# Two more halves of the adaLN vectors summed on VectorE, in two other places of the stream, with six stream buffers in place of seven

## The chip, the cores and the metric

The kernel runs on one core of one Trainium2 chip. The metric is the device time of one execution in microseconds (us), as a median of several runs; lower is better.

## What is computed

One decoder block on 256 tokens of width 2048, in float32. What matters here is the conditioning ahead of it and the order of the large products:

```
cond = silu(c)
ada = cond @ w_ada + b_ada                    # 2048 -> 6 * 2048
sh1, sc1, gt1, sh2, sc2, gt2 = split(ada, 6)
u = rmsnorm(h) * (1 + sc1) + sh1
proj = u @ w_in                               # queries, keys/values, gates, S5 input, merge gates
y_a = sparse attention(...)
y_b = GLU(S5 scan(...))
h = h + gt1 * ((g_a * y_a + g_b * y_b) @ w_out)
u2 = rmsnorm(h) * (1 + sc2) + sh2
h = h + gt2 * (relu(u2 @ w_up)^2 @ w_down)
out = rmsnorm(h)
```

sc1 and sh1 are wanted first, since the whole projection waits for u. gt1, sh2 and sc2 (the "later vectors") are wanted only when w_out's product ends. gt2 has code of its own, which the change doesn't touch.

## The kernel before, in words

**The stream.** All weights pass through one list of *units*. A unit loads one tile `raw` of 128x1024 float32 (512 KB) on SyncE's DMA queue and then does something with it. There are RAW = 7 such buffers, and the load of a unit is issued RAW units ahead (two fewer while the S5 outputs run, which borrow two buffers). `run_units` (L244) walks the list; its order is the order of work on every engine's queue.

**Main units** (`gemm=True`) split the weights in two: ScalarE copies `raw` to `hi` (L117), VectorE writes `lo = raw - hi` (L120), and TensorE does three products per tile of weights (L316, L318, L319, or L923 to L925 for the values, where weights and activations change sides). TensorE's part of a unit is put in its queue SPLIT = 2 main units later. `hi` and `lo` have three buffers each.

**Units without a split** (`gemm=False`) are the adaLN vectors and the compression of keys and values. For the later vectors there are six halves of 1024 columns: half h is vector h // 2 (gt1, sh2, sc2), columns 1024 * (h % 2) on. A half takes 16 tiles in either of two ways:

- `ada2_pe_units` (L1046, TensorE): the tiles come in pairs. For each pair, 16 products of 128 columns (L1060) go into one PSUM bank, ScalarE copies the bank to a stage, and after every fourth pair four transposes (L1069) and a sum on VectorE finish 512 columns.
- `ada2_units` (L973, VectorE): each tile, 128 rows of w_ada, is multiplied by the 128 values of `cond` and added to a 128x1024 accumulator, one instruction of VectorE a tile (a `tensor_scalar` for the first, L124, then 15 `scalar_tensor_tensor`, L129). At the end TensorE sums over the partitions (L991), ScalarE copies, and TensorE transposes (L1000).

Which half goes which way stands in a tuple, and how many tiles go into which stage in a list:

```
RAW, HI, LO = 7, 3, 3
ADA2 = [0, 16, 16, 16, 32, 16]
ADA_PE = (0, 1, 3, 4, 5)
...
units += weave(proj_units(C_GA, d_g, 0, AF.Tanh, 0.5, True), some())
```

`some()` hands out the next ADA2 tiles, `weave` spreads them over the main units of a stage. The six stages before are: the end of the values with the S5 inputs (mark E), the merge gates of A (ga), the queries (q), the merge gates of B (gb), the GLU (glu), the output product (out). So half 0 lies in ga, half 1 in q, half 2 (on VectorE) in gb, halves 3 and 4 in glu, half 5 in out.

**What lies around the change.** The first pass goes over w_in in five chunks of rows, since u comes in pieces; each chunk has four passes (two of S5 input, one of compressed keys/values, one of keys), and each pass ends with four sums of a PSUM bank into SBUF on VectorE (`RX<-A`, for the keys `st<-A` with a store to DRAM on ScalarE's queue). The last chunk has 16 main units. Then come the values (mark vs; 16 main units, 8 units of compression woven in), and from mark E on, with the last six of them and the gate unit, the S5 inputs.

*Background generators* put other work between units. Those that matter: `p2` (S5 operands, copies at L741, up to 8 units ahead of vs, counted in units), `xw` (x^T stored to DRAM on GpSimd's queue, at vs - 20), `cmp` (sums for the compression, at vs - 2), `lam` (`s5_lambda`, twelve 128x1024 operations of VectorE, after vs), `keep` (stores of d_c on SyncE's queue, L786), `stk` and `in` (S5 inputs: SBUF to SBUF copies on GpSimd's queue, L809, products L835, and four ScalarE copies a step), and `attn` (attention, during glu).

Of the kernel before, what the change touches and what calls it, by code (L numbers as in the profile page):

```python
# [23 lines left out]
    0, 2048, 3072, 3584, 4096, 4608, 5120, 5168, 7216, 9264)  # L24
A_SH1, A_SC1, A_GT1, A_SH2, A_SC2, A_GT2 = (i * D for i in range(6))

RAW, HI, LO = 7, 3, 3
SPLIT = 2
ADA2 = [0, 16, 16, 16, 32, 16]
ADA_PE = (0, 1, 3, 4, 5)  # L30
SCAN_END = 0.4
ATTN_WAIT = 5
AS0, AS1 = 2, 13
# [48 lines left out]
def block_kernel(ctx, tc, cst_in, x, c, w_ada, b_ada, g_mix, w_in, w_ck2, pe_ck,  # L82
# [21 lines left out]
    def big4():  # L104
        return sp.tile([128, 1024], FT, tag="s4", name="s4", bufs=2)
# [79 lines left out]
    units = []  # L185
# [231 lines left out]
    def first_pass_units(ci):  # L417
        k0, k1 = chunks[ci]
        res = []
        for g in PASS:  # L420
            def finish(b, ps, g=g):
                acc = part[g][:, b * 512:(b + 1) * 512]
                if ci == 0:
                    copy(acc, ps)
                elif ci < len(chunks) - 1 or g < 3:
                    tt(acc, ps, acc, OP.add)
                else:
                    st = stage()
                    tt(st, ps, acc, OP.add)
                    A.dma_start(out=d_k[:, 2 * b:2 * b + 2, :], in_=st.rearrange("p (k t) -> p k t", k=2))  # L430
            kw = dict(halves=l_keys) if g == 3 else {}
            col0 = (C_SSM, C_SSM + 1024, C_KC, 0)[g]
            res += gemm_pass(w_in[0], col0, list(range(k0, k1)), 1024, True, True, (uh, ul), BA, finish, joint=J_P1 if ci >= J_P1C else 1, **kw)
        return res
# [476 lines left out]
    def vs_units():  # L911
        made = {}

        def run(u, kt):
            if kt == 0:
                made["b"] = [bank(t) for t in BA]
            lo = u.lo
            for t in range(2):
                xh, xl = uh[:, kt, t * 128:t * 128 + 128], ul[:, kt, t * 128:t * 128 + 128]
                for s in range(2):  # L920
                    o = made["b"][2 * t + s]
                    at = slice(512 * s, 512 * s + 512)
                    PE.matmul(out=o, lhsT=xh, rhs=u.hi[:, at], start=kt == 0, stop=False)  # L923
                    PE.matmul(out=o, lhsT=xl, rhs=u.hi[:, at], start=False, stop=False)
                    PE.matmul(out=o, lhsT=xh, rhs=lo[:, at], start=False, stop=kt == 15)  # L925
                    if kt == 15:
                        st = stage()
                        copy(st, o)
                        A.dma_start(out=d_v[:, t, s, :], in_=st)
        return [Unit([(lambda r: r, l_vals[kt])], lambda u, k=kt: run(u, k)) for kt in range(16)]  # L930

    def gate_unit():
        def run(u):
            ps = bank("T0")
            h3 = u.hi.rearrange("p (k n) -> p k n", n=48)
            l3 = u.lo.rearrange("p (k n) -> p k n", n=48)
            for kt in range(16):
                o = ps[0:48, 0:256]
                PE.matmul(out=o, lhsT=h3[:, kt], rhs=uh[:, kt, :], start=kt == 0, stop=False)
                PE.matmul(out=o, lhsT=h3[:, kt], rhs=ul[:, kt, :], start=False, stop=False)  # L940
                PE.matmul(out=o, lhsT=l3[:, kt], rhs=uh[:, kt, :], start=False, stop=kt == 15)
            st = stage()
            A.activation(out=st[0:48, 0:256], in_=ps[0:48, 0:256], func=AF.Tanh, scale=0.5)

            def fin():
                p2 = bank("T0")
                for t in range(2):
                    PE.transpose(p2[:, 48 * t:48 * t + 48], st[0:48, t * 128:t * 128 + 128], ident[0:48, 0:48])
                ts(gates.rearrange("p i n -> p (i n)"), p2[:, 0:96], 0.5, OP.mult, 0.5, OP.add)
            defer(1, fin)  # L950
        return [Unit([(lambda r: r[:, 0:768], l_gate)], run, width=768)]
# [23 lines left out]
    def ada2_units(vec, half, tag):  # L975
        off = (A_GT1, A_SH2, A_SC2, A_GT2)[vec] + 1024 * half
        hold = {}

        def run(u, kt):
            if kt == 0:  # L980
                hold["a"] = big4()
                ts(hold["a"], u.raw, cond[:, 0:1], OP.mult)
            else:
                stt(hold["a"], u.raw, cond[:, kt:kt + 1], hold["a"], OP.mult, OP.add)
            if kt == 15:
                defer(FIN_GAP, fin1)

        def fin1():
            ps = bank(tag)
            for i in range(2):  # L990
                PE.matmul(out=ps[32 * i:32 * i + 32, :], lhsT=ones32, rhs=hold["a"][:, 512 * i:512 * i + 512],  # L991
                          start=True, stop=True, tile_position=(0, 32 * i))
            hold["s"] = stage()
            copy(hold["s"][0:64], ps[0:64, :])
            defer(FIN_GAP, fin2)

        def fin2():
            ps = bank(tag)
            for j in range(4):
                PE.transpose(ps[:, 64 * j:64 * j + 64], hold["s"][0:64, 128 * j:128 * j + 128], ident[0:64, 0:64])  # L1000
            k0 = 16 * vec + 8 * half
            bk = 32 + 16 * vec + 8 * half
            tt(ada2[:, k0:k0 + 8].rearrange("p (h j) -> p h j", h=2),
               ps[:, 0:256].rearrange("p (j h n) -> p h j n", j=4, h=2)[:, :, :, 0],
               bada_c[:, bk:bk + 8].rearrange("p (h j) -> p h j", h=2), OP.add)
            if vec == 2 and half == 1:
                stt(s2, sc2_c, 1.0, gmlp_c, OP.add, OP.mult)
        return [Unit([(lambda r: r, w_ada[0, kt * 128:(kt + 1) * 128, off:off + 1024])],
                     lambda u, k=kt: run(u, k), gemm=False) for kt in range(16)]


# [604 lines left out]
    def weave(main, extra, tail=6, head=0):  # L1616
        if not extra:
            return list(main)
        res, ie = [], 0
        for i, u in enumerate(main):  # L1620
            res.append(u)
            want = max(0, min(len(extra), (i + 1 - head) * len(extra) // (len(main) - tail - head)))
            res += extra[ie:want]
            ie = want
        return res

    with tc.manual_schedule():
        units += ada1_units(0)
        for ci in range(1, len(chunks)):
            units += merge(ada1_units(ci), first_pass_units(ci - 1))  # L1630
        units += first_pass_units(len(chunks) - 1)
        e2 = []
        for h in range(6):
            if h in ADA_PE:
                e2 += ada2_pe_units(h // 2, 2 * (h % 2)) + ada2_pe_units(h // 2, 2 * (h % 2) + 1)
            else:
                e2 += ada2_units(h // 2, h % 2, "T12")
        marks["vs"] = len(units)
        vs = vs_units()
        units += vs[:VA] + weave(vs[VA:VB], compress_units(), 0) + vs[VB:VC]  # L1640
        marks["E"] = len(units)
        dist = iter(np.cumsum([0] + ADA2))

        def some(a=[next(dist)]):
            lo_, a[0] = a[0], next(dist)
            return e2[lo_:a[0]]
        units += weave(vs[VC:] + gate_unit(), some())
        marks["ga"] = len(units)
        units += weave(proj_units(C_GA, d_g, 0, AF.Tanh, 0.5, True), some())
        marks["q"] = len(units)  # L1650
# [88 lines left out]
```

## Time and profile before

| | |
|---|---|
| median of 3 runs | 1750.05 us (1748.83 to 1750.44) |
| profiled execution, its own time | 1755.79 us |
| its span | 1754.0 us |
| read from HBM | 386.93 MB |
| stream queue (SyncE) | 386.54 MB in 129392 packets |

The span is the time from the first to the last instruction of the profiled execution; its time holds 1.8 us around it. TensorE's busy time counts a matmul from its start to a modelled end, so that matmuls overlap and a stretch that reads as full can hold more or fewer of them: the pitch between their starts says what one costs. An engine that is idle beside a full TensorE costs nothing.

### The profile page before, as it was taken

To read this page: it belongs to the slowest core of one execution; us is meant where nothing else is said; L and a number is where in the kernel's file an instruction comes from. 1 tells how busy PE (TensorE), PEld (TensorE's weight loads), DVE (VectorE), ACT (ScalarE), POOL (GpSimd) and SP (SyncE) were. 2 spreads that over 40 slices of the span, in tenths; PEclk is the share of its full clock that TensorE was granted. 3 is DMA by queue.
4 is the path that set the end of the run, shared out by engine and by line. 5 is a ranking of instruction groups with operands and counts; after the bars stand their busy time and mean duration, and the time that the engine had idled before them with its cause. 6 is when DMAs were issued, how large, how long until landed. Compare 5 with 4: busy or idle time off the path is not lost.

```text
span 1754.0 us, 32823 instructions
## 1 busy us (share of the span) xinstructions
PE 1693.2 (97%) x13246; PEld 1490.6 (85%) x13246; DVE 1150.7 (66%) x2120; ACT 841.7 (48%) x1376; POOL 30.5 (2%) x53
## 2 busy tenths in 40 slices
PE   6999999889999999999999999999999999999997
PEld 4788899679999988888889999888888888887885
DVE  4868567438887876666656576666666655556555
ACT  3443443563333467655554444444444455555554
POOL 1000000210000000000000000000000000000000
PEclk8999999999999999999999999999999999999999
DMA  8988756848888877966658747777777655555562
GB/s 331 341 274 315 253 185 194 290 137 281 305 261 286 256 219 240 308 240 215 206 190 279 272 151 232 228 247 239 237 239 240 195 182 190 193 193 180 194 194 93
DMA packets 136408, 408.06 MB, mean 233 GB/s; under 512 B 13936, under 2 KB 18512, under 8 KB 135232
## 3 DMA queue, kind: packets, MB, share of 16 engines
q1 hardware_dynamic: 129392, 386.54, 66.4%
q0 software_dynamic: 2032, 10.72, 1.7%
q10 hardware_dynamic: 4832, 8.70, 1.3%
q8 instruction: 104, 1.70, 0.4%
q14 instruction: 48, 0.39, 0.1%
HBM read 386.93 MB, written 16.88 MB: 230 GB/s over the span
## 4 chain that ended last, share of the span: by engine, by line
PE 86%; DVE 5%; ACT 5%; DMA 2%; issue 1%; ACTq 0%; SPq 0%; DVEq 0%
PE A L316 12%; PE A L344 12%; PE A L318 12%; PE A L319 12%; PE A L1603 6%; PE A L1601 6%; PE A L1602 6%; PE A L345 6%; PE T L1060 2%; DVE lo L120 2%; PE T L368 1%; ACT hi L117 1%; ACT RX L117 1%; DMA raw<-in_l_ada_dram 1%; DMA raw<-in_l_vals_dram 1%
## 5 line engine op out<-in xcount | busy, mean ns | idle before, releaser
L120 DVE TENSOR_TENSOR lo<-raw,hi 128x1024 fp32r<-128x1024 f32 (+1 forms) x497 | 605.6, 1222 | 413.3 <-ACT hi L117 409.2
L117 ACT ACTIVATE hi<-raw 128x1024 fp32r<-128x1024 f32 (+1 forms) x497 | 523.7, 1056 | 540.1 <-PE A L318 189.0
L316 PE MATMUL A<-RU,hi 128*128 128x256 f32 x1664 | 486.0, 292 | 3.3 <-ACT RU L411 1.5
L319 PE MATMUL A<-RU,lo 128*128 128x256 f32 x1664 | 474.3, 285 | 1.2 <-DVE lo L120 1.2
L318 PE MATMUL A<-RU,hi 128*128 128x256 f32 x1664 | 474.2, 285 | 0.0
L316 PEld LDWEIGHTS A<-RU,hi 128*128 128x128 f32 x1664 | 322.4, 194 | 26.4 <-issue 20.1
L319 PEld LDWEIGHTS A<-RU,lo 128*128 128x128 f32 x1664 | 322.2, 194 | 1.8 <-DVE lo L120 1.7
L318 PEld LDWEIGHTS A<-RU,hi 128*128 128x128 f32 x1664 | 322.6, 194 | 0.3 <-DVE RU L129 0.2
L344 PE MATMUL A<-RU,hi 128*128 128x512 f32 x896 | 317.3, 399 | 0.0
L345 PE MATMUL A<-RU,lo 128*128 128x256 f32 x896 | 251.4, 281 | 0.0
L344 PEld LDWEIGHTS A<-RU,hi 128*128 128x128 f32 x896 | 168.2, 188 | 41.7 <-issue 0.7
L1603 PE MATMUL A<-lo,RB 128*128 128x512 f32 x512 | 199.7, 390 | 1.4 <-DVE lo L120 1.4
L1601 PE MATMUL A<-hi,RB 128*128 128x512 f32 x512 | 200.2, 391 | 0.8 <-ACT hi L117 0.8
L1602 PE MATMUL A<-hi,RB 128*128 128x512 f32 x512 | 199.2, 389 | 0.0
L345 PEld LDWEIGHTS A<-RU,lo 128*128 128x128 f32 x896 | 169.2, 189 | 1.0 <-issue 1.0
L1603 PEld LDWEIGHTS A<-lo,RB 128*128 128x128 f32 x512 | 96.1, 188 | 22.7 <-DVE lo L120 2.7
L1601 PEld LDWEIGHTS A<-hi,RB 128*128 128x128 f32 x512 | 96.1, 188 | 21.0 <-ACT hi L117 1.4
L1602 PEld LDWEIGHTS A<-hi,RB 128*128 128x128 f32 x512 | 96.1, 188 | 19.6
L117 ACT ACTIVATE RB<-RX 128x256 fp32r<-128x256 f32 x160 | 64.1, 402 | 27.4 <-DVE RX L129 27.4
L316 PE MATMUL A<-RB,hi 128*128 128x256 f32 x256 | 73.6, 287 | 1.4 <-ACT RB L117 1.2
L318 PE MATMUL A<-RB,hi 128*128 128x256 f32 x256 | 72.7, 284 | 0.2
L319 PE MATMUL A<-RB,lo 128*128 128x256 f32 x256 | 72.3, 283 | 0.0
(255 smaller groups left out, 1737.7 us busy)
## 6 DMA issues: line engine op xcount, KB each, us to landing
raw<-in_l_ada_dram SPq DMA_DIRECT2D x144, 512.0 KB, 5.0
raw<-in_w_in_dram SPq DMA_DIRECT2D x144, 512.0 KB, 4.8
raw<-in_w_up_dram SPq DMA_DIRECT2D x128, 512.0 KB, 3.9
raw<-in_w_down_dram SPq DMA_DIRECT2D x128, 512.0 KB, 4.7
raw<-in_w_ada_dram SPq DMA_DIRECT2D x48, 512.0 KB, 3.9
raw<-in_w_glu_dram SPq DMA_DIRECT2D x32, 512.0 KB, 5.2
raw<-in_w_out_dram SPq DMA_DIRECT2D x32, 512.0 KB, 6.4
raw<-in_l_keys_dram SPq DMA_DIRECT2D x16, 512.0 KB, 4.8
```

The source lines that it names most:

```text
L117: A.activation(out=out, in_=in_, func=AF.Copy, scale=scale)
L120: V.tensor_tensor(out=out, in0=a, in1=b, op=op)
L316: PE.matmul(out=o, lhsT=w.hi[:, at], rhs=xh, start=first and j % 2 == 0, stop=False, skip_group_check=True)
L318: PE.matmul(out=o, lhsT=w.hi[:, at], rhs=xl, start=False, stop=False, skip_group_check=True)
L319: PE.matmul(out=o, lhsT=w.lo[:, at], rhs=xh, start=False, stop=last, skip_group_check=True)
L344: PE.matmul(out=o, lhsT=u.hi[:, at], rhs=xp, start=k0 + t == 0, stop=False, skip_group_check=True)
L345: PE.matmul(out=o[:, 0:256], lhsT=u.lo[:, at], rhs=xp[:, 0], start=False, stop=k0 + t == 15, skip_group_check=True)
L368: PE.matmul(out=ps[q:q + 32, :], lhsT=cond[:, t0 + t:t0 + t + 1].to_broadcast([128, 32]), rhs=r[:, t, :], start=t0 == 0, stop=t0 == 12, ti ...
L1060: PE.matmul(out=ps[q:q + 32, 0:128], lhsT=cond[:, kt:kt + 1].to_broadcast([128, 32]), rhs=r[:, kt % 8, :], start=kt < 4, stop=kt >= 12, ti ...
L1601: PE.matmul(out=o, lhsT=xh, rhs=w.hi[:, at_], start=k == 0, stop=False)
L1602: PE.matmul(out=o, lhsT=xl, rhs=w.hi[:, at_], start=False, stop=False)
L1603: PE.matmul(out=o, lhsT=xh, rhs=w.lo[:, at_], start=False, stop=k == 63)
```

## The change

- ADA_PE becomes (2, 3, 5): halves 0, 1 and 4 are summed on VectorE, and 2, 3 and 5 on TensorE. Before, half 2 alone was on VectorE.
- ADA2 becomes [16, 16, 16, 16, 16, 16, 0] with one more stage ahead: half 0 lies in the last chunk of the first pass, half 1 at mark E, 2 in ga, 3 in q, 4 in gb, 5 in glu, none in out. At E and in the last chunk the tiles are spread up to the stage's last main unit (the 0 as `weave`'s tail).
- The accumulator gets a buffer of its own (`acc`, 4 KB a partition), and RAW becomes 6.

```diff
-RAW, HI, LO = 7, 3, 3
+RAW, HI, LO = 6, 3, 3
 SPLIT = 2
-ADA2 = [0, 16, 16, 16, 32, 16]
-ADA_PE = (0, 1, 3, 4, 5)
+ADA2 = [16, 16, 16, 16, 16, 16, 0]
+ADA_PE = (2, 3, 5)
...
-                hold["a"] = big4()
+                hold["a"] = sp.tile([128, 1024], FT, tag="acc", name="acc")
...
-        units += first_pass_units(len(chunks) - 1)
...
+        dist = iter(np.cumsum([0] + ADA2))
+
+        def some(a=[next(dist)]):
+            lo_, a[0] = a[0], next(dist)
+            return e2[lo_:a[0]]
+        units += weave(first_pass_units(len(chunks) - 1), some(), 0)
         marks["vs"] = len(units)
...
-        units += weave(vs[VC:] + gate_unit(), some())
+        units += weave(vs[VC:] + gate_unit(), some(), 0)
```

Since the marks are positions in the list, `xw` now falls into the last chunk (20 units ahead of vs are ten main units there, and were the whole chunk and four more units), and `p2` is spread over 96 units in place of 80.

**VectorE, third pass of the last chunk** (keys; `lo<-raw,hi` is a main unit's split, `st<-A` the end of a pass, `acc<-raw,cond,acc` one tile of half 0, L741 the operand copies). Before:

```order
L120 TENSOR_TENSOR lo<-raw,hi 128x1024 x4
L120 TENSOR_TENSOR st<-A_2986,RX 128x512
L120 TENSOR_TENSOR st<-A_2987,RX 128x512
L120 TENSOR_TENSOR st<-A_2988,RX 128x512
L120 TENSOR_TENSOR st<-A_2989,RX 128x512
L120 TENSOR_TENSOR lo<-raw,hi 128x1024 x4
```

and with the change:

```order
L120 TENSOR_TENSOR lo<-raw,hi 128x1024
L741 COPY s_1864<-RX 64x4x2x16 x2
L129 SCALAR_TENSOR_TENSOR acc<-raw,cond,acc 128x1024
L741 COPY s_1864<-RX 64x4x2x16 x2
L120 TENSOR_TENSOR st<-A_2941,RX 128x512
L120 TENSOR_TENSOR st<-A_2942,RX 128x512
L120 TENSOR_TENSOR st<-A_2943,RX 128x512
L120 TENSOR_TENSOR st<-A_2944,RX 128x512
L120 TENSOR_TENSOR lo<-raw,hi 128x1024
L129 SCALAR_TENSOR_TENSOR acc<-raw,cond,acc 128x1024
```

One accumulation now stands behind every split of the chunk, and operand copies reach into it.

**VectorE from mark E on.** Before (`RX<-T` behind L1190 is the compression's last but one step, `t` the scan's first):

```order
L120 TENSOR_TENSOR lo<-raw,hi 128x1024
L1190 COPY RX<-T_3690 128x4x15
L120 TENSOR_TENSOR lo<-raw,hi 128x1024 x6
L120 TENSOR_TENSOR lo<-raw,hi 128x768
L120 TENSOR_TENSOR lo<-raw,hi 128x1024
L120 TENSOR_TENSOR t_4092<-RX,l2r 128x128
```

and with the change:

```order
L124 TENSOR_SCALAR acc<-raw,cond 128x1024
L129 SCALAR_TENSOR_TENSOR acc<-raw,cond,acc 128x1024
L120 TENSOR_TENSOR lo<-raw,hi 128x1024
L129 SCALAR_TENSOR_TENSOR acc<-raw,cond,acc 128x1024 x2
L120 TENSOR_TENSOR lo<-raw,hi 128x1024
L129 SCALAR_TENSOR_TENSOR acc<-raw,cond,acc 128x1024 x2
L120 TENSOR_TENSOR lo<-raw,hi 128x1024
L129 SCALAR_TENSOR_TENSOR acc<-raw,cond,acc 128x1024 x3
```

Two or three accumulations stand between one split and the next.

**SyncE's queue, the loads for mark E** (one piece of the difference; L786 are the stores of d_c):

```order
-L211 DMA raw<-in_l_vals_dram 128x1024 x2
+L211 DMA raw<-in_l_vals_dram 128x1024
+L211 DMA raw<-in_w_ada_dram 128x1024
 L786 DMA d_c<-RX 128x1024
-L211 DMA raw<-in_l_vals_dram 128x1024 x3
+L211 DMA raw<-in_w_ada_dram 128x1024
+L211 DMA raw<-in_l_vals_dram 128x1024
+L211 DMA raw<-in_w_ada_dram 128x1024 x2
+L211 DMA raw<-in_l_vals_dram 128x1024
+L211 DMA raw<-in_w_ada_dram 128x1024 x2
```

The tiles of half 1 come between those of the values, two for one.

## Rows read from the trace of the kernel before

**Rows 1.** The page, part 1: busy time of each engine.
```profile
PE 1693.2 (97%) x13246; PEld 1490.6 (85%) x13246; DVE 1150.7 (66%) x2120; ACT 841.7 (48%) x1376; POOL 30.5 (2%) x53
```
**Rows 2.** Stretches: from:to, length, busy time (instructions) by engine, clock, DMA share, GB/s.
```profile
44.00:88.00 44.00, 40.69 (x376) 33.00 (x374) 37.87 (x119) 18.15 (x30) 0.00 (x0) 0.92 0.96 341
130.00:244.00 114.00, 110.50 (x1177) 96.35 (x1176) 75.36 (x115) 50.18 (x89) 1.44 (x2) 1.00 0.77 265
244.00:284.50 40.50, 39.37 (x355) 38.88 (x354) 25.94 (x33) 15.92 (x22) 2.14 (x4) 1.00 0.62 197
284.50:318.85 34.35, 32.05 (x249) 27.01 (x248) 34.09 (x43) 10.11 (x16) 0.26 (x1) 1.00 0.59 199
...
336.00:377.00 41.00, 36.70 (x339) 30.02 (x338) 6.32 (x6) 34.22 (x70) 8.68 (x16) 1.00 0.53 173
...
720.00:900.00 180.00, 174.59 (x1565) 149.10 (x1565) 117.84 (x363) 98.84 (x305) 0.56 (x1) 0.98 0.68 235
900.00:1040.00 140.00, 135.51 (x1276) 131.16 (x1275) 88.93 (x144) 66.89 (x107) 1.09 (x2) 0.98 0.67 226
```
**Rows 3.** TensorE in order of time: start, length, instruction, xcount.
```profile
494.67 0.28 PE L319 MATMUL A<-RU,lo 128*128 128x256 f32 x1
494.88 1.08 PE L1060 MATMUL T<-raw,cond 128*32 128x128 f32 x32
495.89 0.38 PE L316 MATMUL A<-RU,hi 128*128 128x256 f32 x1
496.12 0.28 PE L318 MATMUL A<-RU,hi 128*128 128x256 f32 x1
496.23 0.28 PE L319 MATMUL A<-RU,lo 128*128 128x256 f32 x1
```
**Rows 4.** Stretches of line L1060 alone (columns: TensorE and its weight loads).
```profile
700.00:900.00 200.00, 17.29 (x512) 12.98 (x512) 0.98 0.70 239
900.00:990.00 90.00, 8.64 (x256) 6.49 (x256) 1.00 0.76 268
```
**Rows 5.** TensorE by line: shapes, xcount | busy us, mean ns | idle before.
```profile
L1069 PE MATMUL T<-cst,s 128*128 128x128 f32 x40 | 6.0, 274 | 0.7 <-ACT s L117 0.7
...
L991 PE MATMUL T<-s,cst 128*32 128x512 f32 x4 | 1.1, 604 | 0.0
L1000 PE MATMUL T<-cst,st 64*128 64x64 f32 x4 | 0.5, 235 | 0.0
```
**Rows 6.** VectorE on the staging tiles: xcount, ns min/median/max, first and last start.
```profile
L129 DVE SCALAR_TENSOR_TENSOR s<-raw,cond,s x45: 1275/1278/1285, 638.2 to 1364.7; 128x1024 f32<-128x1024 f32 x45
L741 DVE COPY s<-RX x32: 210/222/242, 156.1 to 249.9; 64x128 f32<-64x128 f32 x32
...
L124 DVE TENSOR_SCALAR s<-raw,cond x3: 744/750/754, 636.4 to 1210.8; 128x1024 f32<-128x1024 f32 x3
```
**Rows 7.** VectorE in order of time (in brackets: idle before, and what ended it).
```profile
244.18 2.85 DVE L120 TENSOR_TENSOR RX<-A,RX 128x512 f32<-128x512 f32 x4 [2.48 <-PE A L319]
...
273.30 0.69 DVE L120 TENSOR_TENSOR st<-A,RX 128x512 f32<-128x512 f32 x1 [2.53 <-DMA d_k<-st]
...
294.91 2.46 DVE L120 TENSOR_TENSOR RX<-A,RX 128x512 f32<-128x512 f32 x4
```
**Rows 8.** TensorE in order of time, start of the values.
```profile
314.24 0.50 PE L925 MATMUL A<-lo,RU 128*128 128x512 f32 x1 [1.61 <-DVE lo L120]
```
**Rows 9.** DMA issues from 44 to 88 us: xcount, KB each, median us to landing.
```profile
raw<-in_l_ada_dram SPq DMA_DIRECT2D x17, 512.0 KB, 6.8
```
**Rows 10.** DMA from 320 to 345 us: rate in 40 slices, and issues.
```profile
GB/s 111 354 269 413 387 302 347 380 328 203 262 236 236 282 295 406 406 347 360 269 282 282 275 302 328 397 403 416 403 419 419 400 379 403 418 418 385 410 321 52
...
raw<-in_l_vals_dram SPq DMA_DIRECT2D x7, 512.0 KB, 12.2
```
**Rows 11.** DMA issues from 244 to 295 us.
```profile
raw<-in_w_in_dram SPq DMA_DIRECT2D x8, 512.0 KB, 4.5
```
**Rows 12.** TensorE's waits from 700 to 900 us: total, times, longest.
```profile
PE T L1265 <- ACT RX L1257: 1.4, 1, 1.4
```

More of the change, by code (lines that the diff above doesn't have):

```diff
@@ L1641, in block_kernel @@
         marks["E"] = len(units)
[L1642 to L1646, printed above, removed]
-        units += weave(vs[VC:] + gate_unit(), some())
+        units += weave(vs[VC:] + gate_unit(), some(), 0)
         marks["ga"] = len(units)
```

## The prediction

> **What bounds the kernel now.** I read the busy times first: TensorE is busy for 97% of the span and no other engine for more than 66% [rows 1]. So a microsecond of TensorE's work that goes is a microsecond gained wherever TensorE really has no gaps, and VectorE has room only where its own row says so. That is why the stretches come next [rows 2]. In the GLU and attention (720 to 900 us) TensorE is busy 174.59 of 180, in the output product (900 to 1040) 135.51 of 140: bound by TensorE. In the last chunk of the first pass and the start of the values it is another picture: VectorE is busy 25.94 of 40.5 us from 244 to 284.5, and then 34.09 of 34.35 up to 318.85, that is, full. TensorE waits there for `lo`, 1.61 us at 314.24 [rows 8], and has gaps of 2.3 us in all (34.35 less 32.05). From 336 to 377 (S5 inputs) ScalarE is the busiest after TensorE (34.22 of 41) and VectorE nearly idle (6.32). So the change takes work from where TensorE bounds and puts it once where VectorE has a lot of room, and once where it has some, just ahead of a place where it has none.
>
> **TensorE's work that goes.** A half on TensorE is 8 pairs. A pair pushes the next matmul of a main unit from 494.67 to 495.89 us; the pitch between matmuls around it is 0.12 (496.12, 496.23), so one costs 1.10 us [rows 3]; busy time says 1.08 (17.29 for 512 instructions, 32 to a pair) [rows 4]. Each half ends in two groups of four transposes: 6.0 us for ten groups, so 0.60 a group [rows 5]. Two halves go: 16 x 1.10 + 4 x 0.60 = **20.0 us**. They go from glu (16 pairs become 8) and from out (8 become none); ga and q keep one half on TensorE each, gb one on VectorE. Both places are bound by TensorE, so I count all of it. ScalarE's 16 copies behind the pairs go too, off the path.
>
> **TensorE's work that comes.** A half on VectorE ends in sums over partitions and transposes, 1.1 + 0.5 = 1.6 us [rows 5]; two come, 3.2 us. The one of half 0 falls into the start of the values and those gaps, the other into the start of ga. I take **+2.0**, between 1.6 and 3.2.
>
> **Last chunk and start of the values (244 to 318.85).** Half 0 is one instruction of 0.75 us and 15 of 1.28 [rows 6], 19.95 us; the first stands ahead of the end of the chunk before, so 19.2 fall in. The operands, spread over more units, bring 8 more copies of 0.22 us, 1.8 [rows 6], which leave the stretch ahead. VectorE had 25.94 + 34.09 = 60.0 us of work in 74.85 [rows 2]; now it has 81.0, and 6.2 don't fit even if every gap is filled. Not all can be: at 273.30 it stood 2.53 us for a store [rows 7]. On the other hand, TensorE may run up to two main units behind the splits, and can take some lag. Bounds: the three accumulations behind the third pass meet a VectorE without gaps, so 3 x 1.28 = 3.8 at the least; all 21.0 at the most. I take **+7**, nearest to the 6.2 that the busy times give: 15 accumulations of a kind that is known, beside gaps that are known.
> The stream: the chunk takes 50.7 us before (244.18 to 294.91) [rows 7], at 197 GB/s [rows 2], 10.0 MB. 16 tiles of 0.524 MB and the 2.1 MB of x^T, now stored here, make it 20.5 MB. At 341 GB/s, which the stream held from 44 to 88 us [rows 2], that is 60 us, less 9 for the six tiles that have landed when the chunk begins: 51, under the 57.7 that VectorE allows. I take 0, between 0 and 2.3 (60 less 57.7).
>
> **S5 inputs (336 to 377).** VectorE has 34.7 us free for 16 accumulations of 20 us: hidden, by a stage that ScalarE and TensorE hold up. The DMAs are less sure: 173 GB/s in 41 us is 7.1 MB [rows 2], and 8.4 MB come. 15.5 MB need 45.4 us at 341 GB/s (+4.4), and 37 at the 413 or so that single slices reach [rows 10] (+0). Behind each load on SyncE's queue stands the next, and a late tile of half 1 holds up VectorE and with it the next split. I take **+3**, between 0 and 8 (4.4, and one more wait of 3.6, as half of what a landing there exceeds the others by: 12.2 less 4.5, [rows 10, 11]). The Trainium skill (DMA: Bandwidth & Descriptors, Specifications) puts HBM at some 358 GB/s a core, which speaks against this place too: by it the 15.5 MB need 43.3 us, +2.3 in place of my +3, and the sum would be -7.2. The slices over 400 show that here it is no ceiling for a microsecond or two; no row shows it broken for longer.
>
> **Six buffers.** From 44 to 88 us the DMAs are busy 0.96 of the time [rows 2], and a tile lands after 6.8 us [rows 9], against 4.5 where the queue is not full [rows 11]. A third of that is queueing, more than the seventh of the tiles that goes, so the rate should hold: 0 at the least, 44 / 7 = 6.3 at the most if the rate goes with the number of tiles. I take **+1.5** for this and for the S5 outputs, where four units of lead remain.
>
> **The sum:** -20.0 + 2.0 + 7 + 0 + 3 + 1.5 = **-6.5 us**. The profiled execution took 1755.79 us, so it would be 1749.3; the median of the runs lies 5.7 lower (1750.05), and on it I forecast **1743.5 us**. A measurement of this kernel tells some 0.2%, 3.5 us, from no change.
>
> **Rivals.**
> *B, all but hidden.* Splits run two main units ahead of TensorE, some 5.8 us by the pitch of 0.12 and 24 matmuls a unit [rows 3], and TensorE's gaps in the values absorb what remains: the 7 becomes 0, the 3 and 1.5 together 1. -20 + 2 + 1 = -17: 1733. For it: 14.8 us of gaps in the stretch. Against it: the gaps lie ahead of the full part, and VectorE works in order.
> *C, the stream binds, and it is slower.* Place: the last chunk, where half 0 doubles the loads a main unit. Six tiles turn round in the time of a landing and a hold (split copy and `lo`, taken as twice a pass of 1.28 us over a tile, [rows 6]). With a landing of 12.2 us, as at 320 to 345 us [rows 10], where other queues' DMAs run beside the stream as x^T's store now does here, a unit takes 14.8 / 6 = 2.46 us; the 26 units beyond the first six take 64, against 47 in the forecast (57.7 / 32 a unit). +17: -6.5 + 17 = +10.5, 1760.5. It decides from a landing of about 10 us: then 26 units take 6.5 us more and all is lost. For it: landings of 12.2 do occur. Against it: the stretch from 130 to 244, two loads a main unit as well, runs at 265 GB/s with TensorE at 110.50 of 114 [rows 2].
> *D, glu gives back half.* The pairs filled TensorE's time while attention's chain of VectorE and ScalarE ran; with half of them gone it waits more, and 5 of glu's 10 us are lost: -1.5, 1748.5, no change. Against it: in 200 us TensorE waited for the weights of attention once, 1.4 us [rows 12].
> *E, the change doesn't do what it says.* Then nothing moves: 1750. The order of instructions above shows the accumulations in place, so this is small.
>
> **Chances.** The forecast 0.55; of it 0.09 within 0.2%, where the terms at the chunk and at E come out some 3 us dearer. B 0.14, C 0.17, D 0.12, E 0.02. Faster: 0.46 + 0.14 = 0.60; within 0.2%: 0.09 + 0.12 + 0.02 = 0.23; slower: 0.17. The range reaches from B, 1733, to 1757, which leaves out the upper part of C and the far side of B, under 2 in 10.
>
> **What would show it.** Right: L1060 with 768 instructions in place of 1280; the stretch from 700 to 1040 shorter by some 20 us; VectorE without gaps from about 250 to 325, and TensorE's gaps there grown from 2.3 to some 9 us; the S5 inputs a few us longer, with ScalarE's copies waiting for tiles of the values. Wrong: waits for w_ada's tiles on VectorE in the chunk and landings over 10 us there (C); a chunk as long as before (B); glu shorter by much less than 10 us (D); or a loss ahead of 130 us, which would be the sixth buffer alone.

## The result and the profile after

The change takes 1767.04 us (median of 4 runs, 1765.61 to 1773.85), the kernel before on the same chip 1750.24: a ratio of **1.0093, 95% interval [1.0074, 1.0111]**. It is slower, by some 16 us, where 6.5 us less was forecast; it also lies above the forecast's range, which ended at 1757. The profiled execution took 1767.39 us, its span 1765.6.

TensorE has the work taken away that was to go. The busy times of the changed kernel, part 1 of its page:

```profile
PE 1684.7 (95%) x12734; PEld 1483.0 (84%) x12734; DVE 1187.7 (67%) x2146; ACT 840.9 (48%) x1362; POOL 30.6 (2%) x53
```

Against [rows 1] 512 instructions and 8.5 us of busy time are gone, and VectorE has 37 us more. TensorE also stands idle for longer. Stretches of the changed kernel (last chunk, start of the values, GLU, output product, three pieces of 10 us, and two shorter ones inside these; columns as in [rows 2]):

```profile
248.90:315.04 66.14, 56.65 (x527) 54.64 (x525) 53.44 (x69) 23.66 (x37) 2.15 (x4) 0.95 0.78 268
315.04:347.00 31.96, 27.48 (x206) 20.45 (x205) 28.15 (x34) 11.98 (x23) 4.92 (x9) 1.00 0.64 215
...
755.20:902.80 147.60, 142.10 (x1138) 121.30 (x1138) 101.91 (x321) 84.15 (x267) 0.00 (x0) 0.98 0.57 191
902.80:1081.20 178.40, 172.42 (x1366) 167.43 (x1365) 119.52 (x198) 88.36 (x141) 1.66 (x3) 0.98 0.58 190
...
280.00:290.00 10.00, 4.46 (x57) 4.21 (x57) 6.46 (x10) 1.77 (x3) 2.15 (x4) 0.81 0.78 264
290.00:300.00 10.00, 10.00 (x75) 10.00 (x74) 5.95 (x6) 3.06 (x4) 0.00 (x0) 0.85 0.76 256
...
410.00:420.00 10.00, 6.88 (x34) 6.50 (x35) 4.86 (x14) 4.57 (x6) 0.00 (x0) 0.66 0.54 187
...
288.00:292.50 4.50, 4.50 (x23) 4.50 (x22) 3.44 (x3) 0.95 (x2) 0.00 (x0) 0.50 0.83 252
413.60:418.50 4.90, 4.90 (x23) 4.90 (x24) 3.58 (x11) 1.12 (x2) 0.00 (x0) 0.50 0.40 118
```

GLU and output product in the kernel before, between the same marks:

```profile
724.80:882.50 157.70, 152.38 (x1400) 128.94 (x1400) 102.44 (x324) 85.47 (x275) 0.00 (x0) 0.98 0.67 230
882.50:1067.80 185.30, 180.72 (x1630) 174.33 (x1629) 120.33 (x201) 90.10 (x149) 1.66 (x3) 0.98 0.68 228
```

In GLU and output product TensorE's busy time fell by 18.6 us, so elsewhere it grew by some 10. In the last chunk it was 49.60 before and is 56.65 now: there are 89 instructions more, 80 of them of two more operand blocks, and the clock is 0.95 in place of 1.00.

In the last chunk TensorE has gaps of 9.5 us (66.14 less 56.65), but VectorE isn't full there: 53.44 of 66.14 (before: 36.20 of 50.7). In one piece of 10 us neither is busy for even two thirds. Both wait for something else.

Where the time went, stage by stage, between the two profiled executions. The borders are the first sum that ends the chunk before [rows 7], the one that ends the last chunk, the gate unit's last product (L939), the first and last L1215 of attention, and the first L344 of u2's product:

| stage | before | after | difference |
|---|---|---|---|
| ahead of the last chunk | 244.18 | 248.90 | +4.7 |
| last chunk | 50.7 | 66.1 | +15.4 |
| values, S5 inputs, gate unit | 86.5 | 92.9 | +6.4 |
| ga, q, gb, start of glu | 343.4 | 347.3 | +3.9 |
| glu | 157.7 | 147.6 | -10.1 |
| out | 185.3 | 178.4 | -6.9 |
| up, down, end | 686.2 | 684.4 | -1.8 |

The sum is +11.6. (On medians the loss is larger: the profiled execution of before was 5.7 us over its median.) The gains are there; the loss lies ahead of 420 us. Not every row is the change's: the 18 profiled kernels end their last stage in 684 or 686 us whatever the edit, so the -1.8 is no gain, and of two kernels with the same list ahead of the chunk one can reach it some us later than the other (operands_early at 242.52, all_four_mended at 247.36).

TensorE's waits in the changed kernel, 240 to 310 us (line waited for, total, times, longest):

```profile
PE T L763 <- ACT k L117: 5.9, 2, 5.5
PE T L752 <- DVE s L741: 2.9, 2, 2.0
PE T L752 <- ACT s L117: 1.4, 1, 1.4
PE T L763 <- ACT RB L117: 1.4, 2, 0.7
```

All four belong to the S5 operands of `p2`, work that isn't part of the products or of the new half. Back from the longest one, on VectorE in order of time:

```profile
280.23 0.45 DVE L741 COPY s<-RX 64x128 f32<-64x128 f32 x2
280.71 1.89 DVE L120 TENSOR_TENSOR st<-A,RX 128x512 f32<-128x512 f32 x3
286.09 0.69 DVE L120 TENSOR_TENSOR st<-A,RX 128x512 f32<-128x512 f32 x1 [3.49 <-DMA d_k<-st]
286.70 1.22 DVE L120 TENSOR_TENSOR lo<-raw,hi 128x1024 fp32r<-128x1024 f32 x1
```

and on ScalarE, at the end of the keys and at the end of the values:

```profile
281.44 5.71 ACTq L430 DMA_DIRECT2D d_k<-st  x4
287.19 0.22 ACT L117 ACTIVATE k<-T 128x64 f32<-128x64 f32 x1 [7.55 <-DVE st L120]
...
405.84 0.60 ACT L117 ACTIVATE st<-A 128x512 f32<-128x512 f32 x1 [0.40 <-ACT st L117]
406.47 0.33 ACTq L929 DMA_DIRECT2D d_v<-st  x1
410.69 0.60 ACT L117 ACTIVATE st<-A 128x512 f32<-128x512 f32 x1 [4.25 <-DMA d_v<-st]
411.32 0.33 ACTq L929 DMA_DIRECT2D d_v<-st  x1
411.69 1.06 ACT L117 ACTIVATE hi<-raw 128x1024 fp32r<-128x1024 f32 x1 [0.40 <-ACT st L117]
412.69 0.38 ACT L943 ACTIVATE st<-T 48x256 f32<-48x256 f32 x1
```

Read it so. The keys end in four sums, each into a staging tile `st`, of which there are three. The fourth sum waits 3.49 us until the first store has left its tile. The four stores stand in ScalarE's queue and each waits for its sum, so the queue is held from 281.44 to 287.15. Behind them stands a small operand copy (`k<-T`, L117), and TensorE's L763 waits 5.5 us for that. In the kernel before there was the same wait for the tile, 2.53 us [rows 7], and the four stores held ScalarE's queue for 4.99 us, but no operand work stood behind them. The values do the same on ScalarE alone: the fourth copy waits 4.25 us, with the next split and the gate unit's copy behind it. In the kernel before that wait reads so:

```profile
380.92 0.60 ACT L117 ACTIVATE st<-A 128x512 f32<-128x512 f32 x1 [1.06 <-DMA d_v<-st]
```

Waits of this kind have a second price, told in the granted clock: 0.81 and 0.85 from 280 to 300 us (in the kernel before 1.00 in the whole chunk) and 0.66 from 410 to 420. Right behind TensorE's two long waits, of 5.5 and 3.75 us, it is 0.50, the lower level of 1.2 GHz, full speed being 2.4. TensorE in order of time behind the second wait:

```profile
413.12 0.45 PE L948 MATMUL T<-cst,st 48*128 48x48 f32 x2 [3.75 <-ACT st L943]
...
414.30 0.41 PE L316 MATMUL A<-RU,hi 128*128 128x256 f32 x1
414.52 0.41 PE L318 MATMUL A<-RU,hi 128*128 128x256 f32 x1
...
420.25 0.28 PE L316 MATMUL A<-RU,hi 128*128 128x256 f32 x1
420.37 0.28 PE L318 MATMUL A<-RU,hi 128*128 128x256 f32 x1
```

From 413.50 to 418.57 us 24 matmuls start 0.21 us apart in place of 0.12, which is some 2.2 us on top of the wait of 3.75.

### The profile page after: what moved, and what is told of

It reads as the page before. It is cut to its first block, busy times and chain, and to the rows that moved or that the text cites. A ratio compares the mean times of both kernels' runs of the same rounds, so it can differ in the third digit from the quotient of the medians.

```text
span 1765.6 us, 31848 instructions
## 1 busy us (share of the span) xinstructions
PE 1684.7 (95%) x12734; PEld 1483.0 (84%) x12734; DVE 1187.7 (67%) x2146; ACT 840.9 (48%) x1362; POOL 30.6 (2%) x53
## 4 chain that ended last, share of the span: by engine, by line
PE 81%; DVE 8%; ACT 4%; DMA 4%; issue 2%; POOL 0%; ACTq 0%; SPq 0%; DVEq 0%; POOLq 0%
PE A L344 12%; PE A L316 12%; PE A L318 11%; PE A L319 11%; PE A L1603 6%; PE A L1601 6%; PE A L1602 6%; PE A L345 6%; DVE lo L120 3%; ACT hi L117 2%; PE T L368 2%; DMA raw<-in_l_ada_dram 1%; PE T L1060 1%; DVE RX L120 1%; DMA raw<-in_w_ada_dram 1%
## 5 line engine op out<-in xcount | busy, mean ns | idle before, releaser
L117 ACT ACTIVATE hi<-raw 128x1024 fp32r<-128x1024 f32 (+1 forms) x497 | 524.0, 1056 | 541.5 <-PE A L318 182.2
L344 PE MATMUL A<-RU,hi 128*128 128x512 f32 x896 | 315.3, 397 | 0.0
L344 PEld LDWEIGHTS A<-RU,hi 128*128 128x128 f32 x896 | 168.0, 188 | 40.4 <-issue 0.7
L117 ACT ACTIVATE RB<-RX 128x256 fp32r<-128x256 f32 x160 | 64.1, 402 | 27.4 <-DVE RX L129 27.4
```

Source lines behind the costliest of these rows:

```text
L117: A.activation(out=out, in_=in_, func=AF.Copy, scale=scale)
L344: PE.matmul(out=o, lhsT=u.hi[:, at], rhs=xp, start=k0 + t == 0, stop=False, skip_group_check=True)
```

## The experiments

Ratios are to the kernel before on the same chip, with 95% intervals. In kernels with edited stores line numbers shift by up to two.

| run | median us | ratio |
|---|---|---|
| the change | 1767.04 | 1.0093 [1.0074, 1.0111] |
| half_in_chunk_only | 1770.34 | 1.0099 [1.0078, 1.0121] |
| half_at_S5_only | 1755.75 | 1.0009 [0.9997, 1.0022] |
| before_six | 1754.96 | 1.0009 [1.0000, 1.0019] |
| operands_early | 1759.14 | 1.0029 [1.0019, 1.0040] |
| keys_in_place | 1763.17 | 1.0067 [1.0040, 1.0093] |
| chunk_cleared | 1771.48 | 1.0108 [1.0091, 1.0125] |
| chunk_loads_no_sums | 1763.84 | 1.0058 [1.0041, 1.0075] |
| S5_half_later | 1752.71 | 1.0002 [0.9993, 1.0011] |
| operands_early_keys_in_place | 1757.86 | 1.0024 [1.0013, 1.0034] |
| all_three_mended | 1757.49 | 1.0026 [1.0013, 1.0038] |
| S5_half_later_keys_in_place | 1752.06 | 0.9995 [0.9985, 1.0005] |
| out_half_on_VectorE | 1752.48 | 0.9997 [0.9986, 1.0008] |
| values_unblocked | 1746.07 | 0.9956 [0.9939, 0.9972] |
| change_values_unblocked | 1760.59 | 1.0038 [1.0023, 1.0054] |
| before_unblocked | 1749.34 | 0.9977 [0.9965, 0.9988] |
| all_four_mended | 1749.70 | 0.9975 [0.9963, 0.9988] |

### Which part of the change

**before_six**: the kernel before with `RAW = 6`.

> The kernel before with six stream buffers in place of seven and nothing else (1750.2 us before, 1767.0 with the change). Theory of the operand chain (the loss of 15 us in the last chunk comes from the operand blocks that now reach into it): six buffers cost at most 2 us, 1750 to 1752. Theory of the full VectorE (the 16 accumulations in the chunk are the cause by themselves): the same, 1750 to 1752. Theory of the six buffers (a late tile here and there): 5 us or more, 1755 and up, lost ahead of 244 us and at the S5 inputs.

**half_in_chunk_only** and **half_at_S5_only**: the change with one of its two halves (the other one on TensorE again):

```diff
-ADA2 = [16, 16, 16, 16, 16, 16, 0]
-ADA_PE = (2, 3, 5)
+ADA2 = [16, 0, 16, 16, 16, 16, 16]
+ADA_PE = (1, 2, 4, 5)
```

for the chunk, and for mark E the same ADA_PE with

```diff
+ADA2 = [0, 16, 16, 16, 16, 16, 16]
```

> Only the half in the last chunk is on VectorE in a new place (half 0 there, half 3 in gb; ga, q, glu and out one half each on TensorE), none at the S5 inputs; six buffers. All theories that place the loss in the chunk: glu gains 10, the chunk and what lies ahead of it lose 17 to 20, 1757 to 1760. Six buffers: the loss goes with the buffers and not with the chunk, so no more than 5 over the kernel with the half at the S5 inputs.

> Only the half at the S5 inputs is on VectorE in a new place (half 0 there, half 3 in gb; ga, q, glu and out one half each on TensorE), none in the last chunk; six buffers. Operand chain and full VectorE alike: glu gains 10, the S5 inputs lose 4 to 6 as in the change's trace, 1744 to 1748. Six buffers: 5 more, 1750 to 1753.

half_in_chunk_only came out slower than any of the expectations, and half_at_S5_only where the theory of the six buffers put it; but before_six shows no such price. Six buffers cost 1.6 us, with an interval from nothing to 3.3; with the half at mark E alone the time stays as it was (1.0009); the chunk's half alone is as slow as the whole change. The loss is the chunk's, but the half at mark E, too, eats the 10 us that it frees: half_at_S5_only takes 5.3 us more than before_six from the end of the chunk to the gate unit's end, and 2.5 more from there to the first L1215.

### The last chunk: operand blocks, key stores, or a full VectorE

**operands_early**: `p2` ends at the same unit, with the same pace, as in the kernel before.

```diff
-LD0, LD1, P10, P11, P1N, IDLE = 8, 12, 12, 8, 69, 3
+LD0, LD1, P10, P11, P1N, IDLE = 8, 12, 12, 24, 69, 3
```

> The change, with the S5 operand blocks ended 24 units ahead of the values in place of 8, that is, at the same unit of the list and at the same pace as before. Operand chain: the gaps of TensorE in front of L763 and L752 in the chunk (10 us in the change's trace) and the low clock behind the longest go, 1753 to 1757. Full VectorE: the accumulations stay, so at most 3 us come back, 1764 to 1767. Six buffers: as full VectorE.

The chunk falls from 66.1 to 61.9 us, and it begins at 242.52 instead of 248.90. This one number is worth two thirds of the loss (1.0093 to 1.0029). It moves two things at once, the place of the blocks in the chunk and the pace ahead of it: of the 11.6 us between the two profiles 4.2 lie in the chunk and 6.4 ahead of it. What remains is the tile that the keys wait for, now 5.46 us:

```profile
279.57 0.69 DVE L120 TENSOR_TENSOR st<-A,RX 128x512 f32<-128x512 f32 x1 [5.46 <-DMA d_k<-st]
```

**keys_in_place**: the keys are summed into their accumulator and stored from there, so that no sum waits for a tile.

```diff
-                    st = stage()
-                    tt(st, ps, acc, OP.add)
-                    A.dma_start(out=d_k[:, 2 * b:2 * b + 2, :], in_=st.rearrange("p (k t) -> p k t", k=2))
+                    tt(acc, ps, acc, OP.add)
+                    A.dma_start(out=d_k[:, 2 * b:2 * b + 2, :], in_=acc.rearrange("p (k t) -> p k t", k=2))
```

> The change, with the keys stored from the accumulator in SBUF into which VectorE adds them, in place of three staging tiles: the fourth sum no longer waits for the first store to land. Theory of the waits in order (ScalarE's copies for the operand blocks stand behind the stores of the keys, and TensorE behind the copies): the gap of 5.5 us in front of L763 and the low clock behind it go, 6 to 9 us less than the change, some 8 to 11 above before. Theory of the full VectorE (the accumulations cost by their time): the wait only moves work, at most 3 us less than the change.

L763's longest wait falls from 5.5 to 2.3 us, the chunk from 66.1 to 62.0, the ratio from 1.0093 to 1.0067. The intervals overlap, and 4.6 us of median are less than the theory wanted (6 to 9) and more than its rival did (3).

**chunk_loads_no_sums**: 15 of half 0's 16 sums on 64 columns in place of 1024.

> The change, with 15 of the 16 products of half 0 in the last chunk made on 64 of their 1024 columns: the loads stay, VectorE's 18 us there go (the rest of half 0's sums is left out). Full VectorE: 8 us or more less than the change. Waits in order: the stores of the keys and the operand blocks still meet, so 5 us or less come back. Theory of the stream (doubled loads in the chunk): 3 us or less come back.

The loads and the order are the change's; the rest of these sums is left out. 1.0058 of 1.0093 remains, with the wait of 5.3 us for `k<-T`. So most of the loss isn't the sums' time, though some 6 us go with them, between the 5 and the 8 that the expectations set apart. The landings are no cause either; DMA issues of the changed kernel from 249 to 315 us:

```profile
raw<-in_w_ada_dram SPq DMA_DIRECT2D x12, 512.0 KB, 5.3
raw<-in_w_in_dram SPq DMA_DIRECT2D x8, 512.0 KB, 4.9
```

against 4.5 in [rows 11]; rival C wanted 10.

**chunk_cleared**: keys in place, operand blocks out of the chunk (`P11 = 32`) and x^T's store earlier in the list (`KX = 36`).

> The change, with the keys stored in place, the operand blocks ended 32 units ahead of the values (wholly ahead of the last chunk), and x^T stored at the same place of the program as before (36 units ahead of the values). Waits in order: what is left in the chunk is VectorE's work, which fits its gaps but for a few us; the kernel comes to within 3 us of before, on either side. Full VectorE: 5 us or more above before, with the chunk 8 us or more longer than its 50 us.

The last of these edits could do nothing in the chunk: x^T's store falls into it only by its place in the list. GpSimd's queue issues it long before, at 156.00 us in the kernel before, at 159.6 here, and in the change at

```profile
172.85 0.54 POOL L492 DMA_DIRECT2D d_xT<-RX  x1
```

The run is a miss, and instructive. Its stretches:

```profile
244.00:264.39 20.39, 17.06 (x127) 16.57 (x121) 11.65 (x18) 8.36 (x13) 0.00 (x0) 0.83 0.49 156
264.39:316.33 51.94, 49.82 (x407) 48.40 (x405) 50.07 (x56) 17.57 (x18) 2.14 (x4) 1.00 0.94 345
```

The chunk itself takes 51.9 us, little more than the 50.7 of before, with VectorE busy for 50.07 of them. (The stream moves 345 GB/s there at a DMA share of 0.94.) But it begins 20 us late: the 90 steps of `p2`, which had 80 units before and 96 in the change, were pressed into 72, and the stretch ahead lost more than the chunk won. In the change the slower pace costs there too, if less: the five profiled kernels with it (half_in_chunk_only, change_values_unblocked, chunk_loads_no_sums, the change, keys_in_place) reach the chunk at 245.2 to 251.1 us, the twelve with the pace of before at 242.5 to 247.4. The means are 247.3 and 244.4, so some 3 us; the two groups overlap, and no kernel that changes the pace alone was run.

### Mark E and the start of ga

**S5_half_later**: half_at_S5_only, with no tile of half 1 behind the first two main units (`weave(..., some(), 0, 2)`).

> As the kernel with the half at the S5 inputs only, with its tiles spread over the last five of the seven main units there, so that none is asked for while d_c is stored and the S5 inputs are copied. Theory of the crowd (the first copies of the S5 inputs wait for a store of the compressed keys that lands late, TensorE waits 4.6 us and its clock falls): 3 to 6 us less than that kernel, 1750 to 1752 where before is 1754. Rival (ScalarE holds the stage up, and tiles late or not cost the same): within 1.5 us of that kernel.

In half_at_S5_only the first S5-input copies waited for the compressed keys' store:

```profile
337.98 5.61 ACT L117 ACTIVATE RX<-T 128x256 f32<-128x256 f32 x12 [4.74 <-DMA d_kc<-RX]
```

Whether half 1's loads made that store late is open: it landed after 7.1 us, 5.4 in before_six, but 6.8 in the kernel before, where ScalarE stood idle 3.71 us in front of these copies for a load of the values.

That wait goes with the later start, but the gain, 1.0009 to 1.0002, is within the intervals, and under 1.5 us, as its rival had it.

**operands_early_keys_in_place**, **all_three_mended** (that and the later start) and **S5_half_later_keys_in_place**: the edits together, in the change and without the chunk's half.

> The change with two edits together: the operand blocks end at the unit and pace of the kernel before (P11 = 24), and the keys are stored from their accumulator. Theory (the loss is a chain of waits in order: operand copies behind accumulations, the four key stores on ScalarE's queue, and the fourth key sum behind the first store): operands_early (1.0029) had one such wait left in the chunk, 5.5 us at the keys' fourth sum; it goes, and this is some 5 us faster: 0.9985 to 1.001, last chunk 55 to 57 us (61.9 there). Rival one (VectorE is simply full in the chunk: 16 sums of 1.28 us don't fit): taking a store's wait out moves it elsewhere, 1.002 to 1.004, chunk 60 us or more. Rival two (the stream): the same as rival one, with landings in the chunk well over 5 us.

> As operands_early_keys_in_place, and half 1 begins two main units later at mark E. Theory: the first S5-input copies no longer wait for the store of the compressed keys (4.6 us of TensorE), of which S5_half_later got back 3 us in its profile: 0.996 to 0.9995. If the S5 inputs are held by the DMAs' rate rather than by that one wait: no different from operands_early_keys_in_place.

> S5_half_later (1.0002; half 1 alone moved, to mark E, nothing in the last chunk, halves 0, 3, 4, 5 on the places of the kernel before) with the keys stored from their accumulator. Theory: without the accumulations in the chunk the keys' fourth sum waits 2.5 us as in the kernel before; that goes, 1 to 3 us: 0.9985 to 1.000. Rival (VectorE is full there, nothing else): there are no accumulations in this chunk, so no difference from 1.0002.

Misses: against operands_early the two further edits gave the change 0.0005 at the most. In operands_early_keys_in_place the chunk takes 58.7 us, between the 55 to 57 of the theory and the 60 of its rival. In all_three_mended the chunk is down to 56.7 us, but from there to the gate unit's end it takes 91.3 us, before 86.5, and to the first L1215 another 348.1, before 343.4. Something at mark E or behind it was still there, in all three kernels.

**values_unblocked**: S5_half_later_keys_in_place with the third and fourth copy of the values in a tile of their own. **change_values_unblocked**: that edit alone in the change. **before_unblocked**: the kernel before with both store edits. **all_four_mended**: all_three_mended with it.

```diff
-                        st = stage()
+                        if t == 1 and s == 0:
+                            made["w"] = big4()
+                        st = made["w"][:, at] if t else stage()
```

> S5_half_later_keys_in_place (0.9995) with the third and fourth copy of the values in a tile of their own, so that no copy waits for a store. (a): ScalarE's wait of 5.4 us and TensorE's of 4.9 us at the start of ga go, and the low clock behind them: 3 to 6 us faster, 0.996 to 0.998. (b): no difference, 0.999 to 1.000.

> The change itself with that one edit (ScalarE's wait of 4.25 us, TensorE's of 3.8 us). (a): 3 to 5 us faster than the change, 1.0065 to 1.008. (b): as the change, 1.0093.

> The kernel before (one half on VectorE, seven buffers, none of the change) with the keys stored from their accumulator and the values' last two copies in a tile of their own. Its waits there are 1.1 us (keys) and 3.1 us (gate unit): (a) 2 to 4 us faster, 0.9975 to 0.999. (b): 1.000.

> The change with every wait in order that was found taken away: operand blocks early, keys in place, half 1 later, values' copies unblocked. If the chunk costs its +7 in VectorE's time and nothing else is left: all_three_mended (1.0026) less 3 to 5 us, 0.9995 to 1.001, that is, no gain from the chunk's half. (b): 1.0026.

All four came out faster, by as much as was expected or more. At the start of ga, S5_half_later_keys_in_place (TensorE's longest wait from 377 to 470 us; a stretch of 10 us):

```profile
PE T L947 <- ACT st L942: 4.9, 1, 4.9
```

```profile
384.00:394.00 10.00, 5.41 (x25) 5.32 (x26) 4.41 (x11) 3.35 (x5) 0.00 (x0) 0.71 0.54 186
```

and the same place in values_unblocked, ScalarE in order of time, TensorE's wait and a stretch:

```profile
379.55 0.60 ACT L117 ACTIVATE s<-A 128x512 f32<-128x512 f32 x1 [0.74 <-ACT st L117]
380.18 0.33 ACTq L930 DMA_DIRECT2D d_v<-s  x1
380.55 0.60 ACT L117 ACTIVATE s<-A 128x512 f32<-128x512 f32 x1 [0.40 <-ACT s L117]
```

```profile
PE T L949 <- ACT st L944: 0.2, 1, 0.2
```

```profile
375.00:395.00 20.00, 19.84 (x180) 17.86 (x179) 16.45 (x43) 10.69 (x17) 0.00 (x0) 1.00 0.90 313
```

The wait is gone, and so is the low clock. In the change, the stage from the gate unit to L1215 falls from 347.3 to 341.3 us by this edit, 6.0 for a wait of 3.8: the wait and the 2.2 us of slow matmuls behind it.

values_unblocked beats both kernels: 0.9956 [0.9939, 0.9972]. Half of that is in before_unblocked, 0.9977, which has no half moved; the half at mark E is worth the other 3.3 us of median (1746.07 against 1749.34). all_four_mended, 0.9975, is 3.6 us slower than values_unblocked. The intervals of these three overlap, so both differences are uncertain; but a gain from the half in the chunk is not to be seen, even with every known wait taken away.

### Is a half on VectorE always worth its 10 us?

**out_half_on_VectorE**: S5_half_later_keys_in_place with `ADA_PE = (1, 2, 4)`, so that half 5, in out, is summed on VectorE too.

> As S5_half_later_keys_in_place, and the half in the output product is summed on VectorE too (16 sums of 1.28 us, VectorE busy 115 of 180 us there) in place of 8 pairs on TensorE. Theory (a half taken from TensorE is worth its 10 us where VectorE has room and no chain of waits runs through it): 8 to 10 us faster than S5_half_later_keys_in_place, less 1 for the end of the half: 0.993 to 0.995. Rival (the clock gives the gain back: TensorE that does less is granted less): within 3 us of it.

A miss: the same time. Two stretches of out in S5_half_later_keys_in_place:

```profile
910.00:940.00 30.00, 28.73 (x302) 27.28 (x302) 18.30 (x28) 15.33 (x26) 0.00 (x0) 1.00 0.77 264
940.00:970.00 30.00, 30.00 (x319) 29.01 (x318) 20.93 (x35) 15.07 (x26) 1.09 (x2) 1.00 0.92 328
```

and with the half on VectorE:

```profile
910.00:940.00 30.00, 27.15 (x200) 24.50 (x199) 23.34 (x33) 13.70 (x20) 0.00 (x0) 1.00 0.77 241
940.00:970.00 30.00, 27.78 (x210) 25.68 (x209) 25.94 (x37) 14.88 (x24) 1.09 (x2) 1.00 0.83 289
```

TensorE's pairs are replaced by gaps, 5.1 us of 60 against 1.3, and by a slower sequence of matmuls: without the six pairs that lay here, 407 of out's own matmuls run in these 60 us where 423 did. The whole stage takes 186.2 us, 185.3 with the half on TensorE, and 178.4 in the change, which has no half there. Each tile of out's products needs a merged operand that VectorE and ScalarE prepare in order, and accumulations stand between those steps. VectorE is not full, 25.94 of 30; that its results yet come later is the likely reason, but not a shown one (TensorE's waits in out for ScalarE's and VectorE's operands are short, 2.0 us in the longest group). The clock is 1.00 in both, so that rival isn't the cause in these stretches. What each accumulation delays was not tried apart.

## Why the prediction was wrong

**TensorE's work that goes, -20.0: right in kind, 3 us too much.** glu gave 10.1 of its 10: TensorE's busy time there fell by 10.3 and its gaps stayed (5.3, now 5.5). (Most kernels with this glu take 147.1 to 147.8 us there, four take 150.1.) out gave 6.9: busy time fell by 8.3, and the gaps grew from 4.6 to 6.0. Rival D, a glu that gives back half, fell; TensorE's wait for the weights of attention is 1.4 us, as in [rows 12]. L1060 has 768 instructions, as forecast.

**Six buffers, +1.5, and ends of the halves, +2.0.** before_six says 1.6 us for the first. The ends lie in the stages around them and were not measured alone.

**Last chunk and start of the values, +7: the step that failed.** Where +7 stood, +17.3 was measured (with half 0's end, which falls there). Here is the stretch from the first border to the start of the fifth split of the values, before and after:

```profile
244.18:317.63 73.45, 70.03 (x583) 64.67 (x583) 58.81 (x73) 24.63 (x32) 2.14 (x4) 1.00 0.61 200
...
248.90:339.62 90.72, 77.82 (x671) 70.17 (x671) 77.92 (x98) 29.53 (x46) 2.15 (x4) 0.96 0.74 253
```

VectorE's work was forecast well: it grew by 19.1 us, and 21.0 were forecast. But the +7 let it fill nearly every gap, 81.0 us of work in 81.85 (74.85 and 7). In the run it stood idle for 12.8 of 90.72. The step counted VectorE's sums against VectorE's gaps, and let the operand copies enter as "8 more copies of 0.22 us, 1.8". Copies were the wrong measure. An operand block is a chain, VectorE (L741), TensorE (L752), ScalarE (`k<-T`), TensorE (L763), each link in an engine's queue in order. Moved into the chunk it stands behind accumulations on VectorE and, on ScalarE, behind four stores that wait for sums that wait for a tile. The change lost 15.4 us in the chunk and 4.7 ahead of it (some 3 by the means of the two groups above). With the chain put back, operands_early is 1.0029. In the chunk itself the 66.1 us become 61.9 with the blocks put back and 58.7 with the keys' stores mended too; so about half of the +15.4 is that chain of waits. Beneath it the price of a full VectorE is there, but was not measured clean. In all_four_mended the chunk takes 58.7 us where values_unblocked takes 49.2, +9.6: 5.1 of it in the first pass, where an operand block still stands (17.6 against 12.5), 4.5 in the other three, with VectorE busy for 50.98 of 58.74. In chunk_cleared, with no operand block, it is 51.9, +2.8 against values_unblocked, which still has one. The +7 lies between: for VectorE's time alone it may have been right. The prediction even named the wait for the store (2.53 us, [rows 7]), but as a gap that VectorE can't fill, not as one that grows and that others queue behind.

**S5 inputs, +3: right only with the waits taken away.** From the end of the chunk to the gate unit's end values_unblocked takes 88.7 us and before_unblocked 85.8: +2.9, the forecast. But there half 1 begins later and the stores are mended. With the change's own order the place costs more, +5.3 in half_at_S5_only, within the range of 0 to 8, and +2.5 behind it. The Trainium skill (DMA: Bandwidth & Descriptors, Specifications), named in the prediction for its 358 GB/s a core, gave +2.3. The traces don't bear that figure out as a ceiling for this core, and the measurement decides: 20 us moved 371 GB/s in the kernel before (720 to 740 us) and 386 in chunk_cleared (290 to 310). [Rows 10] had shown it, too: its 13 slices from the 26th on, 8.1 us, average 405, where the prediction allowed "a microsecond or two". What was missed lies behind: the stores of the values. Their landing, 4.2 us in the kernel before, is 6.4 in the change and 7.4 in S5_half_later_keys_in_place, and so the wait for the tile grew from 1.06 to 4.25 us and more. The prediction asked what a late tile of half 1 would hold up, and not what half 1's tiles would make late. Taking that one wait away gave the change 1.0093 to 1.0038.

**The stream, 0.** The term came out, but one of its parts was wrong: x^T's store, 2.1 MB, counted here and in rival C, is issued 76 us before the chunk begins. (In the range of the S5 inputs half of 12.2 less 4.5 is 3.85, not 3.6; nothing hangs on it.)

**The rivals.** The sign was that of C, a slower kernel, but not its mechanism: landings in the chunk were 5 us, and the time lies above C's 1760.5. No rival had stores that hold staging tiles.

## What to carry to other kernels

When work or transfers are moved into a stretch, list every instruction there that waits for a *store to land* to get its tile back, and what stands behind it on that engine: the new transfers can lengthen that landing, and here a wait of 1 us became one of 4 to 5 that stopped three engines. Such a wait can be worth mending by itself: before_unblocked, with nothing moved, is 0.9977. A background schedule that is counted in units moves, and changes its pace, whenever the units do: pin it before the new work is judged. And an engine's busy share says whether work fits, not whether a chain through that engine is still on time.

## What the runs showed of the hardware

A wait of TensorE cost more than its length. In the change the 3.8 us at the start of ga are followed by 4.9 us at a granted clock of 0.50, with matmuls 0.21 us apart in place of 0.12, and the wait's removal made that stage 6.0 us shorter and the median 9.6 us (0.0055 of 1753 by the ratios; the rest of that is not placed). The kernel before has the same in small: behind 2.69 us of waiting the clock is 0.50 from 386.0 to 388.5 us. The mean granted clock was 0.981 to 0.984 in the runs of the change, 0.987 to 0.991 in those of before_six and of before_unblocked: 0.006 of 1755 us is some 10 us, an estimate that takes the whole time to go with the clock. The low clock is in part the effect of the waits and not a cause beside them. Runs of one kernel go with it as well: half_at_S5_only took 1748.95 us in an execution with 0.989, and its median is 1755.75. So two single profiles can differ by more than the effect looked for (that of values_unblocked, 1741.88 us, is the shortest of its runs, 4.2 under their median), and the verdicts above go by medians.
